# Decay masks added by accumulating DMAs, weight splits on one engine, four decay buffers and a bias table written in four DMAs

## The chip, the cores and the metric

The kernel runs on one core of one Trainium2 chip. The metric is the device time of one execution in microseconds (us); less is better. The instructions of the five engines (PE multiplies matrices, DVE and ACT work on vectors, POOL is the general engine, SP only issues DMAs) and of the DMA queues are put in a fixed order when the kernel is built: a scheduler of the kernel's framework orders each engine's list, and each engine then runs its list from the front and waits on semaphores. An instruction that waits holds up all that stand behind it on its engine.

## The reference

Two layers, each of a feed-forward block, a mixer and a second feed-forward block, on 512 tokens of 1024 features in float32:

```
for l in range(DEPTH):                                   # DEPTH = 2
    x = x + 0.5 * swiglu_ffn(rms_norm(x), w_gate, w_up, w_down)      # inner width 2816
    x = x + hybrid_mixer(rms_norm(x), ...)
    x = x + 0.5 * swiglu_ffn(rms_norm(x), w_gate, w_up, w_down)

hybrid_mixer: proj = h @ w_in, split into three branches; their outputs side by side @ w_out
  mLSTM, 4 heads of 64:   d[t, s] = exp(b[t] - b[s] + i[s] - m[t]) where s <= t, else 0
                          num = (q @ k.T * d) @ v,  h = num / max(|row sum|, exp(-m))
  SSM, 8 heads of 64:     depthwise convolution of 4 taps, then in blocks of 128 tokens
                          seg[l, s] = exp(a[l] - a[s]) where s <= l, else 0
                          y = (C @ B.T * seg) @ x + carried state
  attention, 4 heads:     softmax(q1 @ k1.T + bias) - lam * softmax(q2 @ k2.T + bias), causal
                          bias[h, t, s] = rel_bias[bucket(t - s), h]
```

## The kernel before

A weight arrives as float32 in tiles of 1 MiB named `raw` (two buffers, loaded on SP's queue, L107) and is split into a rounded part `whi` (ACT, L120) and a remainder `wlo` (L121), three buffers each. Each product of a weight block is then three matmuls (L126 to L128) with the activations' parts `xh` and `xl`. The first feed-forward block loads `wgu` (gate and up) and `wdn`; one `wgu` tile gives 48 matmuls.

The mixer's projections come from the tiles `win` (token-major) and `winf` (feature-major). Their splits go through `msplit` (L298): every third one has its subtraction on POOL, the others on DVE.

The attention works on two pairs of heads (p = 0, 1), four blocks of 128 queries and two heads: 16 steps, each with `soft` (logits by PE L523, bias and minimum by DVE L527, exponential by ACT L530, the two softmaxes joined by DVE L534 to L536), `turn` (transposes by PE L544, copied by ACT L546) and `weigh` (PE L555, DVE L559 and L560). At a pair's first step `load_pair` fetches the stacked queries and keys `st` (six DMAs of 256 KB from `qk_dram`, on POOL's queue, L503) and the bias tile T (L509). T is read from `bias_dram`, which `build_bias` (L239) fills once, in the first feed-forward block: a row of 640 values per head, four rows on four partitions, each written 128 times by one DMA on POOL's queue (L252).

The SSM has four decay tiles `sS` (two heads each, 128x1024) and the mLSTM four decay tiles `D`. An `sS` tile is a row of `row_dram` broadcast over the partitions by a DMA on SP's queue (L629), then POOL adds the causal mask `mask8` (L631), ACT takes eight exponentials (L636), DVE multiplies by the products `pG` (L638) and PE uses the tile (L643). A `D` tile is built in `decay` (L736) from a broadcast row `mb`: POOL adds the mask to four diagonal blocks (L742), ACT takes ten exponentials (L745), `scores` multiplies by `q @ k.T` (PE L755, DVE L756), `value` uses it (PE L764). The tiles T of the two pairs, `sS` 0 to 3 and `D` 0 to 3 take turns in one buffer ring, in that order:

```
        def big(name):
            return mp.tile([P, 1280], F32, name=name, tag="big", bufs=2)
```

Between PE's attention instructions the scheduler puts matmuls of projections for which weights are ready; these are called fillers below. The norms of the heads (`rstd`, L142 to L155) are short chains of small DVE operations.

Of the kernel before, what the change touches and what calls it, by code (L numbers as in the profile page):

```python
# [10 lines left out]
F32 = mybir.dt.float32  # L11
# [3 lines left out]
ALU = mybir.AluOpType  # L15
# [4 lines left out]
P = 128  # L20
# [9 lines left out]
NREL = 640  # L30

# columns of the per-feature vectors, per layer
PV_N1, PV_NM, PV_N2, PV_YW, PV_CW, PV_CB, PV_Q, PV_K, PV_N = 0, 8, 16, 24, 32, 64, 72, 73, 74
# columns of the vectors that every partition holds, per layer
BC_GB, BC_AL, BC_D, BC_LAM, BC_N = 0, 16, 24, 32, 160
# columns of the token-major groups of w_in
WIN_Q = KD * 272
WIN_Z, WIN_V, WIN_O = WIN_Q + 4096, WIN_Q + 8192, WIN_Q + 10240
# columns of the constants
# [4 lines left out]
def hybrid_kernel(ctx, tc, aps, phases):  # L44
# [25 lines left out]
    # ---- residual stream, feature-major  # L70
# [29 lines left out]
    # ---- weights: 1 MiB transfers, split into two float32r parts  # L100
# [29 lines left out]
    # ---- norm of the residual: the gain goes into the operand, the rms is divided out after the product  # L130
# [11 lines left out]
    def rstd(ssq, n):  # L142
        # (ssq / n + eps) ** -0.5 in place: a first guess from the exponent's bits, then Newton steps to float32
# [28 lines left out]
    # ---- SwiGLU  # L172
    def ffn(l, which, nxt, first):
        with tc.tile_pool(name=f"g{l}{which}", bufs=1) as gp:
            gh, gl = [], []
            for f in range(KF):
                if f == 0:
                    # gate and up in step, so that the parts of x are not all needed at once
# [22 lines left out]
                if f == 4 and first:  # L201
                    build_bias()
# [30 lines left out]
    # ---- negated bias of the relative positions: row q holds q + 384 - c at column c  # L233
# [5 lines left out]
    def build_bias():  # L239
        with tc.tile_pool(name="bb", bufs=1) as bp:  # L240
            oh = bp.tile([33, NREL], F32, name="oh")
            nc.sync.dma_start(out=oh, in_=aps["oh"])
            rb = bp.tile([33, 4], F32, name="rb")
            dve.memset(rb, NEG)
            nc.sync.dma_start(out=rb[0:32], in_=aps["rel_bias"])
            dve.tensor_scalar(rb, rb, -1.0, None, ALU.mult)
            row = bp.tile([4, NREL], F32, name="row")
            for a, b in ((0, 320), (320, 640)):
                ps = aux()
                pe.matmul(ps[0:4, :b - a], rb, oh[:, a:b], start=True, stop=True)  # L250
                dve.tensor_copy(row[:, a:b], ps[0:4, :b - a])
            pool.dma_start(out=bias_dram, in_=row[:, None, :].broadcast_to([4, P, NREL]))  # L252

    def mixer(l, nxt):
        pvl, bcl = l * PV_N, l * BC_N
        mp = ctx2.enter_context(tc.tile_pool(name=f"mx{l}", bufs=1))
        # slots of 2 and 8 KiB, each with the tiles that take turns in it
# [14 lines left out]
        def t2(name):  # L272
# [3 lines left out]
            # where the stacked queries and keys of the attention were  # L276
# [11 lines left out]
        def big(name):  # L288
            return mp.tile([P, 1280], F32, name=name, tag="big", bufs=2)

        # pairs of token blocks, 256 columns each
# [4 lines left out]
        npiece = [0]  # L296

        def msplit(raw, lo, n):  # L298
            npiece[0] += 1
            return split(raw, lo, n, pool if npiece[0] % 3 == 0 else dve)  # L300

        def token_proj(first, n, mid=None):
            # columns of one group, token-major, all token blocks at once; two blocks of 256 share a bank
# [23 lines left out]
        def feat_proj(i):  # L327
            # 128 columns, feature-major
# [13 lines left out]
        # ================= values of the attention, gates  # L342
# [12 lines left out]
        # difference weight of the attention  # L355
# [19 lines left out]
        # ================= queries and keys of the attention  # L375
# [14 lines left out]
        # the parts of a query over those of a key: one product of depth 96 for high x high + high x low + low x high  # L390
# [12 lines left out]
        # ================= gates: log1p(u) = 2 artanh(u / (2 + u))  # L403
# [17 lines left out]
        # log forget gates and dt * A side by side  # L421
# [10 lines left out]
        # sums up to a token, after it, and over its block  # L432
# [8 lines left out]
        # negated rows of the SSM's sums  # L441
# [16 lines left out]
        # ---- weights of the mLSTM's sources  # L458
        # log weight of source token s for a target block I, and the start value of its running maximum
# [33 lines left out]
        # ================= differential attention, two heads at a time, with negated logits  # L493
# [18 lines left out]
        def soft(n):  # L512
# [19 lines left out]
            # p1 / s1 - lam * p2 / s2, times -s1  # L532
# [38 lines left out]
        # ================= SSM: convolved inputs, feature-major  # L571
        # silu(x) = h * (1 + tanh(h)), h = x / 2: the taps are halved
# [46 lines left out]
        # decay of the SSM inside a block, log weights above the diagonal hidden  # L619
        for g in range(2):  # L620
# [4 lines left out]
            for pr_i in (2 * g, 2 * g + 1):  # L625
# [3 lines left out]
                nc.sync.dma_start(out=both.rearrange("p (h n) -> p h n", n=S), in_=src.broadcast_to([P, 2, S]))  # L629
                # the sources after a target, in its own block  # L630
                pool.tensor_tensor(blocks(both, P), blocks(both, P), mask8, ALU.add)  # L631
# [16 lines left out]
        # states before blocks 1..3, [state, head, 64], and what they give  # L648
# [29 lines left out]
        def head_norm(Y2, name):  # L678
            # rms over each head's 64 columns
# [26 lines left out]
        # gate and norm of the SSM  # L706
# [24 lines left out]
        # ================= mLSTM  # L731
        off = (0, 512, 896, 1152)
# [3 lines left out]
        def decay(h):  # L736
            mb = mp.tile([P, S], F32, name="row", tag="row", bufs=2)
            nc.sync.dma_start(out=mb, in_=row_dram[l, h:h + 1, :].broadcast_to([P, S]))
            D = big("D")
            for j in range(NB):  # L740
                d = slice(off[j], off[j] + P)
                pool.tensor_tensor(D[:, d], mb[:, j * P:(j + 1) * P], cn[:, CN_MSK:CN_MSK + P], ALU.add)  # L742
                for n in range(j, NB):
                    t = slice(off[j] + (n - j) * P, off[j] + (n - j + 1) * P)
                    act.activation(D[:, t], D[:, d] if n == j else mb[:, n * P:(n + 1) * P],  # L745
                                   AF.Exp, bias=G[:, 4 * j + n, h:h + 1], scale=-1.0)
            wD[h] = D

        def scores(h):
            hp = slice((h % 2) * 64, (h % 2) * 64 + 64)  # L750
            D = wD[h]
            for j in range(NB):
# [3 lines left out]
                dve.tensor_tensor(D[:, off[j]:off[j] + n], sp[:, :n], D[:, off[j]:off[j] + n], ALU.mult)  # L756

        def value(h):
# [3 lines left out]
            for n in range(NB):  # L762
                for j in range(n + 1):
                    pe.matmul(pnv[:, n, :], D[:, off[j] + (n - j) * P:off[j] + (n - j + 1) * P], V[:, j, h, :],  # L764
# [41 lines left out]
        # ================= output projection  # L806
# [35 lines left out]
    for n, (kind, l) in enumerate(phases):  # L842
# [3 lines left out]
        if kind == "mx":  # L846
            if n == 0:
                build_bias()
# [9 lines left out]
def _bucket_rows():  # L858
    # one row per bucket, a last one for the positions that the mask hides; column u is relative position 511 - u
# [21 lines left out]
def layout(inp):  # L881
# [6 lines left out]
    def cols(w, n):  # L888
        # [L, K, n*128] -> [L, n, 128 (k), K/128, 128]
# [66 lines left out]
```

## Time and profile before

| | |
|---|---|
| median of 3 runs | 2031.26 us (2027.05 to 2032.02) |
| span of the profiled execution | 2028.7 us |
| own time of the profiled execution beside its span | not given; the span is 2.56 us below the median of the runs |
| PE busy in the span | 1990.6 us (98%) |
| DVE, ACT, POOL busy | 1014.5, 700.9, 110.1 us |
| granted clock of PE, mean | 0.992 of full speed |

The span runs from the first to the last instruction. The stretches spoken of below are the first feed-forward block (to 385 us), mixer 1 (385 to 672 us), the two feed-forward blocks between the mixers (672 to 1388 us), mixer 2 (1388 to 1676 us) and the last feed-forward block (to the end).

### The profile page before, as it was taken

What the parts mean: (1) busy time and instruction counts of PE and PEld (TensorE: products, weight loads), DVE (VectorE), ACT (ScalarE), POOL (GpSimd) and SP (SyncE); (2) the same over time, 40 slices, a digit from 0 to 9 for tenths busy, and PEclk for the clock granted to TensorE, in tenths of its full rate; (3) what the DMA queues carried; (4) which work ended last, traced back from release to release, by engine and by line L of the source; (5) the groups of instructions that cost most, each with busy time, mean ns of one, the idle gap of its engine ahead of it and who ended that gap; (6) DMA issues with size and microseconds to landing.
All of it is one profiled execution on the core that took longest, in us unless ns stands there. A gap on an engine that the chain in (4) does not pass through costs nothing.

```text
span 2028.7 us, 23646 instructions
## 1 busy us (share of the span) xinstructions
PE 1990.6 (98%) x9654; PEld 1662.2 (82%) x9654; DVE 1014.5 (50%) x1659; ACT 700.9 (35%) x1144; POOL 110.1 (5%) x133
## 2 busy tenths in 40 slices
PE   8999999999899999999999999999998999999999
PEld 6878888978788888888888888889787888888887
DVE  6444433478766444443344444333876754444321
ACT  5223222345554333222232332223464533332211
POOL 0000000132210000000000000001222100000000
PEclk9999999999999999999999999999998999999999
DMA  5332222344212222222222222223532022222321
GB/s 177 95 118 83 104 103 85 118 144 127 83 52 81 86 104 85 103 104 83 104 84 103 104 84 104 103 75 122 159 110 88 32 99 89 104 85 103 109 99 62
DMA packets 35064, 200.73 MB, mean 99 GB/s; under 512 B 5179, under 2 KB 5467, under 8 KB 14092
## 3 DMA queue, kind: packets, MB, share of 16 engines
q1 hardware_dynamic: 29756, 185.28, 26.2%
q0 software_dynamic: 5200, 13.95, 2.8%
q8 instruction: 75, 1.23, 0.2%
q14 instruction: 33, 0.27, 0.0%
HBM read 191.56 MB, written 7.65 MB: 98 GB/s over the span
## 4 chain that ended last, share of the span: by engine, by line
PE 92%; DVE 4%; DMA 3%; ACT 1%; issue 1%; SPq 0%; POOL 0%; ACTq 0%; DVEq 0%; POOLq 0%
PE acc L126 16%; PE acc L128 16%; PE acc L127 16%; PE aux L126 12%; PE aux L128 12%; PE aux L127 12%; DMA raw<-wgu 3%; PE aux L764 1%; PE aux L643 1%; PE po L555 1%; PE po L755 0%; PE aux L544 0%; PE aux L523 0%; PE side L755 0%; ACT whi L120 0%
## 5 line engine op out<-in xcount | busy, mean ns | idle before, releaser
L120 ACT CAST whi<-raw 128x1024 fp32r<-128x1024 f32 (+2 forms) x344 | 350.8, 1022 | 994.2 <-PE acc L127 407.3
L121 DVE TENSOR_TENSOR wlo<-raw,whi 128x1024 fp32r<-128x1024 f32 (+1 forms) x326 | 386.2, 1187 | 346.1 <-ACT whi L120 345.6
L126 PE MATMUL acc<-xh,whi 128*128 128x512 f32 x896 | 353.1, 394 | 12.8 <-ACT xh L133 8.2
L127 PE MATMUL acc<-xl,whi 128*128 128x512 f32 x896 | 352.5, 393 | 0.0
L128 PE MATMUL acc<-xh,wlo 128*128 128x512 f32 x896 | 352.3, 393 | 0.1
L126 PE MATMUL aux<-xh,whi 128*128 128x512 f32 x704 | 274.2, 389 | 0.0
L128 PE MATMUL aux<-xh,wlo 128*128 128x512 f32 x704 | 274.1, 389 | 0.0
L127 PE MATMUL aux<-xl,whi 128*128 128x512 f32 x704 | 274.1, 389 | 0.0
L126 PEld LDWEIGHTS acc<-xh,whi 128*128 128x128 f32 x896 | 169.4, 189 | 47.3 <-ACT xh L133 8.2
L128 PEld LDWEIGHTS acc<-xh,wlo 128*128 128x128 f32 x896 | 169.1, 189 | 34.7 <-DVE wlo L121 1.1
L127 PEld LDWEIGHTS acc<-xl,whi 128*128 128x128 f32 x896 | 169.4, 189 | 34.0 <-DVE xl L134 0.4
L207 DVE TENSOR_TENSOR us<-aux,rsb 128x512 f32<-128x512 f32 x88 | 60.8, 691 | 265.7 <-PE aux L128 265.7
L127 PEld LDWEIGHTS aux<-xl,whi 128*128 128x128 f32 x704 | 132.3, 188 | 27.6
L128 PEld LDWEIGHTS aux<-xh,wlo 128*128 128x128 f32 x704 | 132.3, 188 | 27.5
L126 PEld LDWEIGHTS aux<-xh,whi 128*128 128x128 f32 x704 | 132.3, 188 | 27.4
L204 DVE TENSOR_TENSOR gs<-acc,rsb 128x512 f32<-128x512 f32 x88 | 60.8, 691 | 176.4 <-PE acc L128 172.5
L126 PE MATMUL acc<-gh,whi 128*128 128x512 f32 x352 | 138.7, 394 | 0.0
L126 PE MATMUL aux<-gh,whi 128*128 128x512 f32 x352 | 138.7, 394 | 0.0
L128 PE MATMUL acc<-gh,wlo 128*128 128x512 f32 x352 | 138.0, 392 | 0.0
L128 PE MATMUL aux<-gh,wlo 128*128 128x512 f32 x352 | 138.0, 392 | 0.0
L127 PE MATMUL acc<-gl,whi 128*128 128x512 f32 x352 | 136.6, 388 | 0.0
L127 PE MATMUL aux<-gl,whi 128*128 128x512 f32 x352 | 136.6, 388 | 0.0
(265 smaller groups left out, 2668.4 us busy)
## 6 DMA issues: line engine op xcount, KB each, us to landing
raw<-wgu SPq DMA_DIRECT2D x87, 1024.0 KB, 4.8
raw<-wdn SPq DMA_DIRECT2D x44, 1024.0 KB, 4.8
raw<-win SPq DMA_DIRECT2D x12, 1024.0 KB, 4.9
raw<-winf SPq DMA_DIRECT2D x12, 1024.0 KB, 4.9
raw<-wout SPq DMA_DIRECT2D x8, 1024.0 KB, 4.8
st<-qk_dram POOLq DMA_DIRECT2D x24, 256.0 KB, 5.4
qk_dram<-hl POOLq DMA_DIRECT2D x16, 256.0 KB, 3.3
sS<-row_dram SPq DMA_DIRECT2D x8, 512.0 KB, 4.4
```

Of the source, the lines that this page charges most:

```text
L120: act.copy(hi[:, t], raw[:, lo:lo + n])
L121: eng.tensor_tensor(lw[:, t], raw[:, lo:lo + n], hi[:, t].bitcast(F32), ALU.subtract)
L126: pe.matmul(out, lh, rh, start=first, stop=False)
L127: pe.matmul(out, lh, rl, start=False, stop=False)
L128: pe.matmul(out, ll, rh, start=False, stop=last)
L204: dve.tensor_tensor(gs, pp[0], rsb, ALU.mult)
L207: dve.tensor_tensor(us, pp[1], rsb, ALU.mult)
L555: pe.matmul(po[:, h * 64:(h + 1) * 64], at["a", n][:, j * P:(j + 1) * P], dv[j][:, (2 * p + h) * 64:(2 * p + h + 1) * 64], start=j == 0, s ...
L643: pe.matmul(py[:, j * P + hh * 64:j * P + hh * 64 + 64], sS[:, hh * S + j * P:hh * S + (j + 1) * P], XC[:, j, h * 64:(h + 1) * 64], start= ...
L764: pe.matmul(pnv[:, n, :], D[:, off[j] + (n - j) * P:off[j] + (n - j + 1) * P], V[:, j, h, :], start=j == 0, stop=j == n)
```

## The change

Four things change, and the order of all engines with them. The line numbers of the changed kernel are one to eleven higher than those of before.

1. The buffer ring `big` has four buffers in place of two.
2. All mixer splits have their subtraction on DVE.
3. The mask goes into `sS` and `D` by a DMA on SP's queue that copies it from the constants in SBUF (L631, L748 of the changed kernel), and the row is added to it by a DMA on POOL's queue that accumulates (L632, L749). POOL's 40 additions are gone. `D` has its four diagonal blocks side by side at the front now, so the multiplication in `scores` is one operation for the diagonal block and one for the rest: 7 in place of 4 for a head. The broadcast row `mb` is still loaded for the other blocks.
4. The bias table is written by four DMAs of one head each, called for at the tiles f = 3, 5, 7 and 9 of the first feed-forward block (before: one DMA, called for at f = 4), from the same four partitions.

```diff
+NBIG = 4
...
-                if f == 4 and first:
-                    build_bias()
+                if first and 3 <= f <= 9 and f % 2:
+                    build_bias(f // 2 - 1)
...
-            pool.dma_start(out=bias_dram, in_=row[:, None, :].broadcast_to([4, P, NREL]))
+    bias_row = const.tile([4, NREL], F32, name="bias_row")
...
+        pool.dma_start(out=bias_dram[h:h + 1], in_=bias_row[h:h + 1, None, :].broadcast_to([1, P, NREL]))
...
-            return mp.tile([P, 1280], F32, name=name, tag="big", bufs=2)
+            return mp.tile([P, 1280], F32, name=name, tag="big", bufs=NBIG)
...
         def msplit(raw, lo, n):
-            npiece[0] += 1
-            return split(raw, lo, n, pool if npiece[0] % 3 == 0 else dve)
+            return split(raw, lo, n)
...
-                nc.sync.dma_start(out=both.rearrange("p (h n) -> p h n", n=S), in_=src.broadcast_to([P, 2, S]))
-                # the sources after a target, in its own block
-                pool.tensor_tensor(blocks(both, P), blocks(both, P), mask8, ALU.add)
+                nc.sync.dma_start(out=blocks(both, P), in_=mask8)
+                pool.dma_start(out=both.rearrange("p (h n) -> p h n", n=S), in_=src.broadcast_to([P, 2, S]),
+                               accum_op=ALU.add)
...
+            nc.sync.dma_start(out=blocks(D[:, 0:S], P), in_=cn[:, None, CN_MSK:CN_MSK + P].broadcast_to([P, NB, P]))
+            pool.dma_start(out=D[:, 0:S], in_=row_dram[l, h:h + 1, :].broadcast_to([P, S]), accum_op=ALU.add)
             for j in range(NB):
-                d = slice(off[j], off[j] + P)
-                pool.tensor_tensor(D[:, d], mb[:, j * P:(j + 1) * P], cn[:, CN_MSK:CN_MSK + P], ALU.add)
...
-                dve.tensor_tensor(D[:, off[j]:off[j] + n], sp[:, :n], D[:, off[j]:off[j] + n], ALU.mult)
+                dve.tensor_tensor(D[:, at_(j, j)], sp[:, :P], D[:, at_(j, j)], ALU.mult)
+                if n > P:
+                    t = slice(off[j], off[j] + n - P)
+                    dve.tensor_tensor(D[:, t], sp[:, P:n], D[:, t], ALU.mult)
```

In POOL's list the four bias DMAs stand one behind the other, and only the first has something to wait for (the row on the four partitions). PE's small matmuls that make this row stand 48 matmuls earlier than before.

**PE, the second pair of heads in mixer 1's attention.** A row is an instruction: its line, its output and inputs by the program's names, the shape of what streams, and how often it stands there. `st` are the stacked queries and keys, `pt` a softmax, `aT` its transpose, `acc` a projection's bank. Before, near the pair's second query block:

```order
L544 MATMUL aux<-cn,pt 128x128
L523 MATMUL aux<-st 128x256 x2
L127 MATMUL acc<-xl_98,whi 128x512
L128 MATMUL acc<-xh_90,wlo 128x512
L555 MATMUL po<-dv_2602,aT 128x64
L126 MATMUL acc<-xh_91,whi 128x512
L127 MATMUL acc<-xl_99,whi 128x512
L128 MATMUL acc<-xh_91,wlo 128x512
L126 MATMUL acc<-xh_92,whi 128x512
```

The same place in the changed kernel:

```order
L545 MATMUL aux<-cn,pt 128x128
L524 MATMUL aux<-st 128x256 x2
L556 MATMUL po<-dv_2605,aT 128x64
L545 MATMUL aux<-cn,pt 128x128 x2
L524 MATMUL aux<-st 128x384 x2
L556 MATMUL po<-dv_2605,aT 128x64 x2
```

In the changed kernel this pair has no fillers from its first logits to its last but one transposes, in mixer 1 alone; mixer 2's two pairs have some between most steps, as before. The fillers that stood there now stand in the first pair of mixer 1 (72 matmuls of three `winf` halves), and the first pair's start has moved behind both `z` projections.

**ACT, the first pair of mixer 1's attention.** `L` are the logits, `nacs` the bias of the SSM's exponentials. Before, the pair's second and third query blocks:

```order
L530 ACTIVATE pt,sm<-L,mx 128x256 x2
L546 COPY aT<-aux 128x256
L587 ACTIVATE rw<-CT_3783 128x512
L530 ACTIVATE pt,sm<-L,mx 128x384
L546 COPY aT<-aux 128x256
```

The same place in the changed kernel:

```order
L531 ACTIVATE pt,sm<-L,mx 128x256
L547 COPY aT<-aux 128x256
L638 ACTIVATE sS<-sS,nacs 128x128 x4
L531 ACTIVATE pt,sm<-L,mx 128x384
L638 ACTIVATE sS<-sS,nacs 128x128
L531 ACTIVATE pt,sm<-L,mx 128x384
L547 COPY aT<-aux 128x256
```

The exponentials of the first two SSM decay tiles have moved between those of the first pair, and those of the third tile between those of the second pair; before, the first decay tile's stood in the second pair and the others behind the attention. The fourth tile's stand behind the attention in both.

**SP, the loads around mixer 1's attention.** `winf` with the mLSTM's queries and keys is loaded in two tiles, `win` here is the mLSTM's values and gate. Before:

```order
L107 DMA raw<-winf 128x2048 x2
L629 DMA sS<-row_dram 128x1024
L107 DMA raw<-win 128x2048 x2
L629 DMA sS<-row_dram 128x1024
L107 DMA raw<-wout 128x2048
L629 DMA sS<-row_dram 128x1024 x2
```

In the changed kernel:

```order
L108 DMA raw<-winf 128x2048
L745 DMA row<-row_dram 128x512
L108 DMA raw<-win 128x2048
L631 DMA sS<-cn 128x8x128 x2
L108 DMA raw<-win 128x2048
L631 DMA sS<-cn 128x8x128
L108 DMA raw<-wout 128x2048
L631 DMA sS<-cn 128x8x128
```

The first two fills with the mask stand behind the load of the values' weights, which needs the `raw` buffer of the first `winf` tile; the third and fourth wait for the buffers of the two pairs' T. In mixer 2 the first two fills stand ahead of the `z` weights and of all `winf` tiles.

## Rows read from the trace of the kernel before

**Rows 1.** The page's head and its busy times by engine.

```profile
span 2028.7 us, 23646 instructions
PE 1990.6 (98%) x9654; PEld 1662.2 (82%) x9654; DVE 1014.5 (50%) x1659; ACT 700.9 (35%) x1144; POOL 110.1 (5%) x133
```

**Rows 2.** Waits of PE: engine, line, releaser, us in total, times, longest.

```profile
PE aux L544 <- DVE pt L536: 7.4, 6, 1.7
...
PE aux L643 <- DVE sS L638: 6.9, 2, 3.5
PE acc L126 <- ACT whi L120: 4.6, 1, 4.6
PE aux L394 <- DVE qk L389: 4.4, 2, 2.2
```

**Rows 3.** Windows: stretch, length, busy us of each engine (instructions), PE clock, DMA share, GB/s.

```profile
385.00:672.00 287.00, 276.33 (x1651) 238.06 (x1650) 199.95 (x453) 139.35 (x312) 50.47 (x53) 0.98 0.31 102
560.00:570.00 10.00, 10.00 (x57) 9.95 (x57) 3.05 (x5) 3.12 (x10) 2.07 (x5) 0.63 0.32 105
672.00:1388.00 716.00, 716.00 (x3174) 591.84 (x3175) 307.06 (x375) 210.38 (x259) 3.61 (x7) 1.00 0.27 95
1560.00:1570.00 10.00, 8.46 (x39) 8.46 (x40) 5.10 (x7) 3.59 (x12) 2.04 (x5) 0.54 0.32 105
```

**Rows 4.** DMA issues of the whole span: count, KB each, median us to landing.

```profile
raw<-wgu SPq DMA_DIRECT2D x87, 1024.0 KB, 4.8
...
st<-qk_dram POOLq DMA_DIRECT2D x24, 256.0 KB, 5.4
...
sS<-row_dram SPq DMA_DIRECT2D x8, 512.0 KB, 4.4
...
bias_dram<-row POOLq DMA_DIRECT2D x1, 1280.0 KB, 56.5
```

**Rows 5.** The chain of work through the bias DMA, 66 to 130 us: start, us, what.

```profile
103.11 22.67 DMA raw<-wgu
```

**Rows 6.** DMA view of 60 to 140 us in 40 slices: busy tenths of 16 engines, GB/s.

```profile
DMA  0086013178222584222222972298222222028308
GB/s 0 0 242 283 0 11 30 20 151 293 26 34 26 75 284 145 56 58 54 57 53 58 245 228 26 26 203 249 23 55 60 65 78 86 0 33 348 143 16 319
```

**Rows 7.** Groups of POOL's instructions by shape, whole span.

```profile
L121 POOL TENSOR_TENSOR wlo<-raw,whi 128x1024 fp32r<-128x1024 f32 x16 | 38.7, 2417 | 147.8 <-ACT whi L120 126.4 <-PE aux L544 21.4
L631 POOL TENSOR_TENSOR sS<-sS,cn 128x1024 f32<-128x1024 f32 x8 | 20.9, 2613 | 48.3 <-DMA sS<-row_dram 44.0 <-DVE rs_q L154 4.2
```

**Rows 8.** Timeline of DVE beside a POOL split that starts at 423.93 us.

```profile
423.76 0.22 DVE L154 SCALAR_TENSOR_TENSOR rs_q<-rs_q,rs_v 128x64 f32<-128x64 f32 x1
424.01 2.40 DVE L155 SCALAR_TENSOR_TENSOR ssq<-rs_q,ssq 128x64 f32<-128x64 f32 x1
```

**Rows 9.** Groups of DVE's, then PE's attention instructions in mixer 1 (385 to 672 us).

```profile
L527 DVE CUSTOM_DVE_ANT_0 L<-aux,T 128x128 f32<-128x128 f32 (+3 forms) x32 | 15.2, 483 | 5.0 <-PE aux L523 4.4 <-ACT pt L530 0.4
L536 DVE SCALAR_TENSOR_TENSOR pt<-pt,ka 128x128 f32<-128x128 f32 (+3 forms) x16 | 10.9, 680 | 0.1
...
L535 DVE SCALAR_TENSOR_TENSOR ka<-sm,lam,ka 128x1 f32<-128x1 f32 x16 | 4.6, 290 | 0.1
...
L527 DVE DVE_READ_ACCUMULATOR2_ANT mx<- 128x1 f32 x32 | 2.6, 82 | 0.0
...
L534 DVE RECIPROCAL ka<-sm 128x1 f32<-128x1 f32 x16 | 2.5, 158 | 0.7 <-ACT pt L530 0.5
...
L555 PE MATMUL po<-dv,aT 128*128 128x64 f32 x80 | 11.6, 276 | 0.2 <-ACT aT L546 0.2
...
L523 PE MATMUL aux<-st 96*128 96x128 f32 (+3 forms) x32 | 9.1, 350 | 0.0
L544 PE MATMUL aux<-cn,pt 128*128 128x128 f32 x40 | 7.2, 279 | 3.7 <-DVE pt L536 3.7
```

**Rows 10.** The chain of work behind mixer 1's attention, 545 to 572 us.

```profile
551.69 2.41 POOL sS L631
```

More of the change, by code (lines that the diff above doesn't have):

```diff
@@ L237, in hybrid_kernel, with build_bias @@
     qk_dram = dram.tile([2, 2, 2, 4, 32, S], F32, name="qk_dram")
[L239 to L251, printed above, removed]
-            pool.dma_start(out=bias_dram, in_=row[:, None, :].broadcast_to([4, P, NREL]))
+    bias_row = const.tile([4, NREL], F32, name="bias_row")
+    def build_bias(h):
+        if h == 0:
+            with tc.tile_pool(name="bb", bufs=1) as bp:
+                oh = bp.tile([33, NREL], F32, name="oh")
+                nc.sync.dma_start(out=oh, in_=aps["oh"])
+                rb = bp.tile([33, 4], F32, name="rb")
+                dve.memset(rb, NEG)
+                nc.sync.dma_start(out=rb[0:32], in_=aps["rel_bias"])
+                dve.tensor_scalar(rb, rb, -1.0, None, ALU.mult)
+                for a, b in ((0, 320), (320, 640)):
+                    ps = aux()
+                    pe.matmul(ps[0:4, :b - a], rb, oh[:, a:b], start=True, stop=True)
+                    dve.tensor_copy(bias_row[:, a:b], ps[0:4, :b - a])
+        pool.dma_start(out=bias_dram[h:h + 1], in_=bias_row[h:h + 1, None, :].broadcast_to([1, P, NREL]))
     def mixer(l, nxt):
@@ L294, in pair @@
             return t, [t[j // 2][:, (j % 2) * 256:(j % 2) * 256 + 256] for j in range(NB)]
-        npiece = [0]
         def msplit(raw, lo, n):
-            npiece[0] += 1
-            return split(raw, lo, n, pool if npiece[0] % 3 == 0 else dve)
+            return split(raw, lo, n)
         def token_proj(first, n, mid=None):
@@ L729, in mixer, with at_ @@
             transpose_out(k, lambda j: YS[:, j, (k - 2) * P:(k - 1) * P], y8[:, k - 2])
-        off = (0, 512, 896, 1152)
+        off = (512, 896, 1152)
+        def at_(j, n):
+            c = j * P if n == j else off[j] + (n - j - 1) * P
+            return slice(c, c + P)
         Ym2, Ym = pair("Ym")
@@ L739, in decay @@
             D = big("D")
+            nc.sync.dma_start(out=blocks(D[:, 0:S], P), in_=cn[:, None, CN_MSK:CN_MSK + P].broadcast_to([P, NB, P]))
+            pool.dma_start(out=D[:, 0:S], in_=row_dram[l, h:h + 1, :].broadcast_to([P, S]), accum_op=ALU.add)
             for j in range(NB):
-                d = slice(off[j], off[j] + P)
-                pool.tensor_tensor(D[:, d], mb[:, j * P:(j + 1) * P], cn[:, CN_MSK:CN_MSK + P], ALU.add)
                 for n in range(j, NB):
-                    t = slice(off[j] + (n - j) * P, off[j] + (n - j + 1) * P)
-                    act.activation(D[:, t], D[:, d] if n == j else mb[:, n * P:(n + 1) * P],
+                    act.activation(D[:, at_(j, n)], D[:, at_(j, n)] if n == j else mb[:, n * P:(n + 1) * P],
                                    AF.Exp, bias=G[:, 4 * j + n, h:h + 1], scale=-1.0)
@@ L763, in value @@
                 for j in range(n + 1):
-                    pe.matmul(pnv[:, n, :], D[:, off[j] + (n - j) * P:off[j] + (n - j + 1) * P], V[:, j, h, :],
+                    pe.matmul(pnv[:, n, :], D[:, at_(j, n)], V[:, j, h, :],
                               start=j == 0, stop=j == n)
@@ L847, in hybrid_kernel @@
             if n == 0:
-                build_bias()
+                for h in range(4):
+                    build_bias(h)
             with ExitStack() as ctx2:
@@ L945 @@
     arrays = layout(inputs)
-    nc = bacc.Bacc("TRN2", target_bir_lowering=False, num_devices=1)
+    nc = bacc.Bacc("TRN2", target_bir_lowering=False, num_devices=1, dynamic_dma_scratch_size=4096)
     aps = {}
```

## The prediction

> **What bounds the kernel now.** The page comes first: PE is busy for 1990.6 of 2028.7 us [rows 1], so the kernel is bound by PE, and an edit on another engine gains only where PE stands idle, at most 38 us in all. PE's waits say where that is [rows 2]: 7.4 us before the attention's transposes (L544) for DVE's L536, 6.9 before the SSM products (L643) for L638, 4.6 once in the first feed-forward block for the cast of a weight, and 4.4 before the transposes of the queries for L389. The windows agree: 716 of 716 us in the blocks between the mixers, 276.33 of 287 in mixer 1 [rows 3]. A second loss doesn't show as idle time: behind the long wait before L643 PE is busy with a granted clock between its two levels of half and full speed, 0.63 (10.00 of 10 us, mixer 1) and of 0.54 (8.46 of 10, mixer 2) [rows 3], which costs 10 x 0.37 = 3.7 and 10 x 0.46 = 4.6 us. Everything below is about these waits, and about new ones like them. The sum is made against the span; the median of the runs lies 2.56 us above it, and I add that at the end.
>
> **Bias table.** The DMA of 1280 KB takes 56.5 us to land, a weight tile of 1024 KB 4.8 [rows 4]. Where it runs alone, the DMA engines are busy for 2 tenths and move 26 GB/s; with a weight load's tail beside it 53 to 58 [rows 6], so the load gets some 30. Loads then take 22.67 us [rows 5], twice in a row (the other 22.80), together 36 us late, and the price was one wait of 4.6: the buffers hold some 31 us of lead.
>
> The table still comes from the same four partitions. Two bounds. If 26 GB/s is the limit of the source, the four DMAs still need 1.31 MB / 26 GB/s = 50 us, but now on more engines, and each weight load meets them in all its parts. PE uses a tile in 48 matmuls of 716 / 3174 = 0.226 us [rows 3], 10.8 us, so it wants 4.6 tiles in those 50 us and gets 50 x 30 GB/s = 1.4; it falls 3.2 x 10.8 = 34 us behind, 3 to 4 more than the lead. Were packets to alternate one for one over the whole 51 us, one tile would come 46 us late: a wait of 15. So 4.6 becomes between 3.5 and 15. If, on the other side, the limit was the few engines, the table clears in some ten us and the 4.6 goes. I take the source limit, and +3, because 26 GB/s is so far below 218 (1 MiB in 4.8 us); bounds -4.6 and +10.
>
> The Trainium skill (SBUF — State Buffer, section on Door 1, the DMA port swizzle) says that partitions 0 to 3 hang on one DMA port of 27.2 GB/s; the 26 of the slices agrees, and by that rule the four DMAs would need 48 us on whatever engines. The same notes (DMA: Bandwidth & Descriptors, how many engines a DMA uses) let the dimension of 4 in the old DMA give four engines and the 128 of the new ones sixteen; the 2 tenths agree with the four, and no run here shows the sixteen. By both rules together the weights are hindered on every engine, which speaks against this edit.
>
> **POOL's tensor work on the way of DVE.** 16 large splits of 2.42 and 8 mask additions of 2.61 us leave POOL [rows 7]. Beside such a split a DVE operation took 2.40 us where its neighbour of the same shape took 0.22 [rows 8], so each can hold DVE for two us, and I put the longest waits before L544, 1.7 us in each mixer, down to that [rows 2]. Against that DVE gets 18 splits of about 1.2, eleven us in each mixer. Before the attention the two about cancel: -0.5 in each mixer, bounds 0 and -2.2 (the wait for L389). In mixer 2's second pair the 1.7 goes.
>
> **Mixer 1, first pair.** The exponentials of the first decay tile now stand between the exponentials of the attention in ACT's list, and whatever is behind them waits until that tile is filled and accumulated. SP's list has the fill behind the load of the values' weights, which needs the `raw` buffer that is freed at about the pair's start. From there: 2 us for that split, 4.8 for the load, some 2 more for the fill beside it (4.4 alone), then an accumulation that no row of before shows. Its nearest rows: the same 512 KB from the same rows by a plain DMA, 4.4, and two of POOL's loads of 256 KB, 10.8 [rows 4]. I take 5.4, nearer to the plain one. That makes 14 us. ACT's list reaches the place behind 27 fillers and the first steps of the pair, some 7.5 us in. ACT waits about 6, PE's instructions behind it a little less: +5, bounds 0 (the load lands earlier) and +8.
>
> **Mixer 1, second pair.** PE's list has no fillers there [the rows of PE's list shown with the change]. A pair costs DVE (15.2 + 10.9 + 4.6 + 2.6 + 2.5) / 2 = 17.9 us, 17 without the held one, and PE (11.6 + 9.1 + 7.2) / 2 = 14.0 [rows 9]; so at least 3 us of idle time, which the fillers covered before. On top, `st` of this pair is loaded when the first pair's last logits are done: six issues of half a microsecond and 5.4 to land [rows 4] against some 27 fillers (6.1 us), so 3 more at the start, and the steps wait for each other's chain. Bounds +3 and +9, taken +6. The displaced fillers are no gain, they filled the first pair. And idle PE was followed by a lower clock above: 2.5 more, bounds 0 and 5.
>
> **The tails.** In both mixers the wait of about 3.45 before L643 ended with POOL's mask addition of 2.41 us [rows 2, 10], behind which stood ACT's and DVE's steps. Three of the four tiles are ready long before now, so it goes, and with it the 3.7 and the 4.6 of low clock. What is late next is D: its buffers come free when the SSM products are done, then fill (4.4 or less), issue and accumulation follow, and ACT's exponentials of the diagonal stand ahead of the copies that PE's state products need. I put 1.5 on it in each mixer, bounds 0 and 4. The split multiplications of `scores` (12 more small DVE operations a mixer) lie beside full PE work; without it, some 0.3 us each.
>
> **Sum.** Mixer 1: -0.5 + 5 + 6 + 2.5 - 3.45 - 3.7 + 1.5 = +7.3. Mixer 2, where fillers and early fills stay: -0.5 - 1.7 - 3.5 - 4.6 + 1.5 + 1 (DVE's added splits between the steps) = -7.8. Bias +3. Together +2.5: a span of 2031.2, a time of 2033.8 us, said as 2034. That is no change by 0.3% (6 us), which is about what a measurement here can tell.
>
> **Rivals.**
> A, the bias on all engines: packets alternate one for one, PE waits 15 instead of 4.6, so 7 above my +3, and a low clock behind it 2: 2043. For it the 22.67 us of a load that met the table on few engines only; against it that the issue may spread the four over time. It decides once a `wgu` load takes over 45 us.
> B, the bias is quick: 4.6 gone instead of +3, 7.6 less, 2026. For it: 26 GB/s may belong to the few engines. Against: a lone weight load gets 13 GB/s from each of sixteen, and the table got 6.5 from each of four or so.
> C, slow accumulation: 10.8 us instead of 5.4 for the first tile puts 5 more on ACT's wait in mixer 1, and some 3 on D in each mixer, 2045. For it, it reads and writes the tile; against, only one tile per mixer is on the path.
> The Trainium skill lists accumulation among what POOL's software queue alone does (DMA: Bandwidth & Descriptors, rules for kernel authors); no row of before shows its time.
> D, the unfilled pair costs nothing: the steps overlap as they did before and the first pair finds its tile ready; -11 in mixer 1's terms, 2023. The 3 us floor speaks against it.
>
> **Chances.** Forecast 0.42 (its own range 2027 to 2041), A 0.18, B 0.18, C 0.15, D 0.07. A and C are slower by over 0.3% for the most part (0.29 of 0.33), B is split about evenly at the bound (0.10 faster), D is faster; of the forecast's own spread 0.09 lies slower and 0.03 faster. So faster 0.20, same 0.42, slower 0.38. The range takes in A, B and nearly all of C: 2020 to 2048.
>
> **What the profile of the changed kernel would show.** Right: four bias DMAs of some 50 us in all and `wgu` loads of over 22 us beside them, with one or two waits of PE of 4 to 8 us by 130 us; no wait of PE at L643's line behind the attention, and clock 1.0 there; idle time of PE inside the second pair of mixer 1, before transposes and logits, and ACT waiting for the accumulation in the first; mixer 2 with some 10 us less idle time than mixer 1. Wrong: bias DMAs that land within 15 us; accumulations beyond 10 us; D's wait behind the SSM over 4 us; or DVE as the releaser in mixer 2's pairs, which would mean that the splits cost more than POOL's hold did.

## The result and the profile after

The changed kernel takes 2050.75 us (median of 4 runs, 2049.02 to 2057.6), the kernel before 2030.55 on the same chip: a ratio of 1.0105, interval 1.0087 to 1.0124. The forecast was no change, 2034 us, in a range to 2048; it is slower by 20 us.

Where the 20 us lie is read off the timelines by marks that both kernels have: DVE's last update of x in a feed-forward block, and its first gate multiplication in the block behind a mixer.

| stage | before, us | after, us | difference | forecast |
|---|---|---|---|---|
| first feed-forward block, to its last update of x | 381.3 | 399.8 | +18.5 | +3 |
| mixer 1, to the next block's first gate | 292.4 | 309.7 | +17.3 | +7.3 |
| two feed-forward blocks between | 711.0 | 711.0 | 0 | 0 |
| mixer 2, to the next block's first gate | 292.5 | 276.9 | -15.6 | -7.8 |
| the rest | 351.5 | 351.5 | 0 | 0 |
| span | 2028.7 | 2048.9 | +20.2 | +2.5 |

All the signs came as forecast, and each of the three sizes was forecast at about half of what was measured or less. The page of the changed kernel, to be held against [rows 1]:

```profile
span 2048.9 us, 23668 instructions
...
PE 1993.5 (97%) x9654; PEld 1663.1 (81%) x9654; DVE 995.9 (49%) x1701; ACT 699.2 (34%) x1144; POOL 48.9 (2%) x94
```

PE is busy for only 2.9 us more than before, so over the whole span the loss is idle time. Its waits (engine, line, releaser, us in total, times, longest; `issue` says that the profile shows nothing that the engine waited for), to be held against [rows 2]:

```profile
PE acc L127 <- ACT whi L121: 22.1, 1, 22.1
...
PE aux L524 <- issue: 6.4, 1, 6.4
PE po L556 <- ACT aT L547: 5.1, 6, 2.3
PE aux L545 <- DVE pt L537: 2.4, 2, 1.6
PE aux L475 <- DVE Gm L467: 1.9, 1, 1.9
```

The three large waits of the mixers in [rows 2] are gone or small. One wait for the cast of a weight has grown from 4.6 to 22.1 us, and there is a new one of 6.4 us before logits. The windows show what that one brings (stretch, length, busy us by engine, clock, DMA share, GB/s). The first and last are mixer 1 and mixer 2 between the marks of the table:

```profile
399.80:709.50 309.70, 290.24 (x1692) 248.10 (x1691) 196.44 (x486) 142.18 (x320) 23.19 (x43) 0.94 0.38 109
540.00:550.00 10.00, 3.60 (x21) 2.75 (x19) 1.68 (x3) 1.93 (x3) 1.67 (x3) 0.82 1.08 238
550.00:560.00 10.00, 7.33 (x30) 6.03 (x29) 5.98 (x30) 6.55 (x26) 0.00 (x0) 0.50 0.37 95
560.00:570.00 10.00, 7.44 (x29) 5.66 (x27) 7.03 (x27) 5.70 (x17) 0.00 (x0) 0.50 0.00 1
570.00:580.00 10.00, 9.27 (x32) 7.51 (x31) 5.60 (x14) 3.00 (x7) 0.89 (x1) 0.50 0.28 66
1420.40:1697.40 277.00, 275.24 (x1692) 238.31 (x1691) 194.38 (x487) 142.06 (x320) 22.93 (x41) 1.00 0.41 122
```

The two mixers between the same marks before:

```profile
381.30:673.70 292.40, 281.73 (x1692) 243.32 (x1691) 204.76 (x465) 142.99 (x320) 53.66 (x62) 0.98 0.32 102
1384.70:1677.20 292.50, 281.79 (x1692) 243.41 (x1691) 204.97 (x465) 143.07 (x320) 53.97 (x62) 0.98 0.31 101
```

From 540 to 550 us PE works for 3.60 us; for the next 30 it runs at a clock of 0.50, the lower of its two levels, with 6 us of gaps in all. Of the 17.3 us that mixer 1 lost, 8.5 are the same number of matmuls that keep PE busy longer, at a mean clock of 0.94 in place of 0.98, and 8.8 are idle time (19.5 against 10.7). Mixer 2 is the opposite: PE is idle for 1.8 us of it, at clock 1.00.

The chain through the bias DMAs and their rows (issues; count, KB each, median us to landing), against [rows 5] and [rows 4]:

```profile
65.67 45.94 DMA raw<-wgu
```

```profile
st<-qk_dram POOLq DMA_DIRECT2D x24, 256.0 KB, 6.2
...
sS<-row_dram POOLq DMA_DIRECT2D x8, 512.0 KB, 6.3
...
D<-row_dram POOLq DMA_DIRECT2D x8, 256.0 KB, 5.0
...
bias_dram<-bias_row POOLq DMA_DIRECT2D x4, 320.0 KB, 32.4
```

and the DMA engines from 50 to 160 us in 40 slices of 2.75 us, against [rows 6]:

```profile
DMA  0373979999997988999995404637003800270037
GB/s 0 69 319 11 32 22 26 28 30 46 54 52 56 67 54 54 53 54 60 70 74 207 191 9 125 256 48 334 0 0 54 334 0 0 66 316 0 0 48 334
```

Here the reader sees where the first loss comes from: from 61 to 108 us all engines are busy, mostly for nine tenths or more, at 22 to 74 GB/s. One weight tile takes 45.94 us in place of 4.8, and the busy share says nothing of what is moved.

### The profile page after: what moved, and what is told of

The parts are those of the page before. It is cut to its first block, busy times and chain, and to the rows that moved or that the text cites. A ratio compares the mean times of both kernels' runs of the same rounds, so it can differ in the third digit from the quotient of the medians.

```text
span 2048.9 us, 23668 instructions
## 1 busy us (share of the span) xinstructions
PE 1993.5 (97%) x9654; PEld 1663.1 (81%) x9654; DVE 995.9 (49%) x1701; ACT 699.2 (34%) x1144; POOL 48.9 (2%) x94
## 4 chain that ended last, share of the span: by engine, by line
PE 93%; DMA 4%; DVE 1%; ACT 1%; issue 0%; SPq 0%; ACTq 0%; POOLq 0%; DVEq 0%
PE acc L127 17%; PE acc L129 17%; PE acc L128 17%; PE aux L127 12%; PE aux L129 12%; PE aux L128 12%; DMA raw<-wgu 2%; PE aux L774 1%; PE po L556 1%; PE po L762 1%; PE aux L645 1%; PE aux L545 0%; DMA sS<-cn 0%; DMA D<-cn 0%; PE aux L524 0%
## 5 line engine op out<-in xcount | busy, mean ns | idle before, releaser
L122 DVE TENSOR_TENSOR wlo<-raw,whi 128x1024 fp32r<-128x1024 f32 (+2 forms) x344 | 407.5, 1187 | 370.0 <-ACT whi L121 369.6
L127 PE MATMUL acc<-xh,whi 128*128 128x512 f32 x896 | 354.0, 395 | 30.4 <-ACT whi L121 22.1
```

What stands on the lines that cost most here:

```text
L122: eng.tensor_tensor(lw[:, t], raw[:, lo:lo + n], hi[:, t].bitcast(F32), ALU.subtract)
L127: pe.matmul(out, lh, rh, start=first, stop=False)
```

## The experiments

**1. One bias DMA again.** In the changed kernel `build_bias` is called at f = 4 alone and writes the table with the old DMA; all else stays.

```diff
-                if first and 3 <= f <= 9 and f % 2:
-                    build_bias(f // 2 - 1)
+                if first and f == 4:
+                    build_bias(0)
...
-        pool.dma_start(out=bias_dram[h:h + 1], in_=bias_row[h:h + 1, None, :].broadcast_to([1, P, NREL]))
+        pool.dma_start(out=bias_dram, in_=bias_row[:, None, :].broadcast_to([4, P, NREL]))
```

> The changed kernel with the bias table written by one DMA at f = 4 as before. Theory: the four DMAs cost 18.5 us in the first feed-forward block, and through the order that the scheduler made with them 17.3 us in mixer 1, while the other three parts gain 15.6 in each mixer. Then this runs in 2050.8 - 18.5 - 17.3 - 15.6 = about 1999 us, with one wait of PE of 4 to 5 us for a weight cast and mixer 1 as short as mixer 2. Rival, the prediction's own: mixer 1 loses by the accumulations and the pair without fillers, whatever the bias does; then only the 18.5 go, about 2032 us.

Measured: 2001.86 us, ratio 0.9859 (0.9844 to 0.9874). PE's waits have the cast at 4.9 us, and both mixers take 277.3 us by the marks (660.6 - 383.3 and 1648.8 - 1371.6):

```profile
PE acc L127 <- ACT whi L121: 4.9, 1, 4.9
PE aux L662 <- ACT bt L659: 1.7, 2, 1.0
PE aux L675 <- ACT st L666: 1.6, 2, 1.0
```

So beside the other three parts the edit of the bias table costs 49 us, and only 16.5 of them (399.8 - 383.3) in the block where it runs; the other three parts alone gain 29 (2031.08 to 2001.86). In the changed kernel the four DMAs had landed by about 111 us, and mixer 1 begins at 400; what the edit changed there is the order. POOL's list has the loads of T ahead of everything else of the mixer in this version, and behind the queries' and keys' loads in the changed one:

```
one DMA:                                  four DMAs:
L256 DMA bias_dram<-bias_row 512x1x640    L256 DMA bias_dram<-bias_row 128x1x640 x4
L462 MEMSET Gm 128x64                     L402 DMA qk_dram<-hl (8 rows)
L469 MEMSET Ps 128x4                      L448 DMA row_dram<-ar 8x512
L510 DMA T<-bias_dram 128x512 x4          L462 MEMSET Gm 128x64
L802 MEMSET V 128x4 x4                    L469 MEMSET Ps 128x4
L402 DMA qk_dram<-hl (8 rows)             L504 DMA st<-qk_dram 32x4x512 x2
L448 DMA row_dram<-ar 8x512               L485 DMA row_dram<-mr 4x128 x4
L504 DMA st<-qk_dram 32x4x512             L504 DMA st<-qk_dram 32x4x512 x4
L485 DMA row_dram<-mr 4x128 x4            L510 DMA T<-bias_dram 128x512 x4
```

In PE's list the pairs of mixer 1 have 91 and 45 filler matmuls between their first and last logits here, as those of mixer 2; in the changed kernel 51 and none. That the scheduler reckoned with a table that is written much later than it is would explain it; the lists show the displacement, its reason inside the scheduler is argued. Four bias DMAs alone do not bring it: in experiments 2 and 4 the pairs of mixer 1 keep their fillers (92 and 38, 91 and 45).

**2. The four DMAs in the kernel before.** `build_bias` and its calls as in the changed kernel, in the kernel before (with the smaller scratch space for DMAs, which makes room for the row).

> The kernel before with the four bias DMAs alone (two buffers, POOL's splits and masks as before; the scratch space for DMAs made smaller as in the changed kernel, since the row needs room). In POOL's list three of the four stand together and the fourth behind the mixer's first split. Theory: three quarters of the bytes hold the weight loads for some 38 us on all engines: a wait of about 34 + 5 - 31 = 8 to 10 us for a cast in place of 4.6, and no change in the mixers beyond 2: 2034 to 2040 us. Rival: if the 22.1 us of the changed kernel came from its DVE splits or its other order, nothing changes here: 2030.

Measured: 2039.06 us, ratio 1.0042 (1.0027 to 1.0057). The wait for the cast is 10.1 us, the other waits are those of [rows 2]:

```profile
PE acc L126 <- ACT whi L120: 10.1, 1, 10.1
...
PE aux L547 <- DVE pt L539: 7.4, 6, 1.7
PE aux L646 <- DVE sS L641: 7.0, 2, 3.5
```

and the slow weight load in the chain of work (start, us, what):

```profile
65.09 33.85 DMA raw<-wgu
```

The loss in the first block needs nothing of the change but these DMAs, and it goes with the bytes that stand together: three of them give 10.1, four gave 22.1. Mixer 1 takes 294.7 us, 2.3 more than before, against the 17.3 more of the changed kernel.

**3. The table from DRAM.** The four rows go to a tile of 10 KB in DRAM, and four DMAs write the table from there. As in experiment 1, `build_bias` is called at f = 4 alone.

```diff
+    bias_small = dram.tile([4, NREL], F32, name="bias_small")
...
-        pool.dma_start(out=bias_dram[h:h + 1], in_=bias_row[h:h + 1, None, :].broadcast_to([1, P, NREL]))
+        pool.dma_start(out=bias_small, in_=bias_row)
+        for k in range(4):
+            pool.dma_start(out=bias_dram[k], in_=bias_small[k:k + 1, :].broadcast_to([P, NREL]))
```

> The changed kernel with the four rows first written to a small tile in DRAM (10 KB) and the table then written by four DMAs from there, DRAM to DRAM, each row broadcast 128 times. Theory (the limit of 26 GB/s is that of the four source partitions): the four DMAs land within some 10 us in all, no wait of PE for a cast, 4.6 us and its low clock better than with one DMA: about 1994 us. Rival (the limit lies with the rows' size, the destination or POOL's queue): they take some 50 us here too, and the wait for the cast is 15 to 22 us: 2010 to 2017.

Measured: 1993.01 us, ratio 0.9817 (0.9801 to 0.9834), the fastest version of the study. The same 1280 KB to the same place, 4.8 us each:

```profile
bias_dram<-bias_small POOLq DMA_DIRECT2D x4, 320.0 KB, 4.8
...
bias_small<-bias_row POOLq DMA_DIRECT2D x1, 10.0 KB, 2.0
```

The first feed-forward block ends at 374.5 us by the marks, 6.9 before the kernel before's. Destination, row size and POOL's queue are out as the limit.

**4. The same four DMAs, far apart.** Each reads a copy of the rows that DVE makes for it; the copies share one place, so each waits for the DMA before.

```diff
+        with tc.tile_pool(name=f"own{h}", bufs=1) as op:
+            own = op.tile([4, NREL], F32, name="own")
+            dve.tensor_copy(own, bias_row)
-        pool.dma_start(out=bias_dram[h:h + 1], in_=bias_row[h:h + 1, None, :].broadcast_to([1, P, NREL]))
+            pool.dma_start(out=bias_dram[h:h + 1], in_=own[h:h + 1, None, :].broadcast_to([1, P, NREL]))
```

> The changed kernel, but each of the four bias DMAs reads its own copy of the rows, which DVE makes when the copy of the DMA before has been read, so that they start far apart (the first near f = 4, the last behind the first feed-forward block). Theory: each still reads one partition at about 26 GB/s and takes 327680 / 26 GB/s = 12.6 us on all engines, but the weights' lead of 31 us covers each by itself: no wait for a cast, about 1994 to 1996 us. Rival: if sixteen engines together draw more than 26 GB/s when nothing is queued behind them, they land in 5 us; if the hold of the engines costs in proportion wherever it lies, waits of some 4 us stand behind each of them: 2010.

Measured: 2013.01 us, ratio 0.9915 (0.99 to 0.9929), 17 to 19 us above the sum that was expected, while the first block, which the experiment was about, came as expected. The DMAs took 13.8 us each, 24 GB/s, and the first block ends at 374.7 us with no wait for a cast: three of them beside weight loads cost nothing. But the fourth was issued at 389.96 us, and the mixer's small tiles, which reuse the copy's place, waited for it (PE's wait, then POOL's):

```profile
PE acc L127 <- DVE cwh L578: 16.8, 1, 16.8
```

```profile
POOL Gm L465 <- DMA bias_dram<-own: 13.3, 1, 13.3
```

That explains 16.8 of the 17 to 19 us; it comes from where the copy lies, not from the DMAs' pace.

**5. Rows on four ports.** The version of experiment 1 with one DMA of the same shape, whose four source rows lie on partitions 0, 4, 8 and 12.

```diff
+                rs = bp.tile([33, 16], F32, name="rs")
+                dve.memset(rs, 0.0)
-                dve.tensor_scalar(rb, rb, -1.0, None, ALU.mult)
+                dve.tensor_scalar(rs[:, 0:16:4], rb, -1.0, None, ALU.mult)
...
-                    pe.matmul(ps[0:4, :b - a], rb, oh[:, a:b], start=True, stop=True)
+                    pe.matmul(ps[0:16, :b - a], rs, oh[:, a:b], start=True, stop=True)
...
-        pool.dma_start(out=bias_dram, in_=bias_row[:, None, :].broadcast_to([4, P, NREL]))
+        pool.dma_start(out=bias_dram, in_=bias_row[0:16:4, None, :].broadcast_to([4, P, NREL]))
```

> The version with one bias DMA (2001.9 us), its four rows now on partitions 0, 4, 8 and 12 in place of 0 to 3; the DMA has the same shape, bytes and engines. Theory: what limits it is a path that the neighbouring partitions 0 to 3 share, some 26 GB/s; the rows on four separate paths give each engine its own rate, at most 4 x 26: 1.31 MB in 13 to 20 us, no wait for the cast, 1995 to 1996 us. Rival: the limit is the four engines or the row's size: it lands after 57 us as before and the wait of 4.9 stays, 2002 us.

Measured: 1993.75 us, ratio 0.9821 (0.9807 to 0.9836). It lands after 18.7 us instead of 57.5, and where no weight load runs beside it (the slices of 2 us from 72 to 76 us and at 86 us) it moves 95 to 105 GB/s, four times the 26 of [rows 6], on the same two tenths of the engines but for its first slice:

```profile
bias_dram<-bias_row POOLq DMA_DIRECT2D x1, 1280.0 KB, 18.7
```

```profile
DMA  0059004269422287000591002750005900028300
GB/s 0 0 74 442 8 0 95 105 162 353 143 106 114 105 227 307 0 0 0 74 401 49 0 0 33 283 217 0 0 0 135 385 4 0 0 33 340 152 0 0
```

This settles the disputed price. The Trainium skill (SBUF — State Buffer, section on Door 1, the DMA port swizzle) gives partitions 0 to 3 one port and partitions 4, 8 and 12 others, 27.2 GB/s each; 26 for one and 105 for four agree with it.

**6. Masks on POOL, with the four DMAs.** The changed kernel with the old code for the masks of `sS` and `D` (and the old layout of `D`), no accumulating DMA. PE's list has mixer 1's second pair without fillers, as the changed kernel's.

> The changed kernel with its four bias DMAs, but the masks added by POOL and no accumulating DMA. Its list for PE has mixer 1's second pair without fillers as the changed kernel's. Theory: mixer 1 loses by that order (late start, no fillers, the wait for the stacked keys, the low clock behind it), not by accumulations: against the same version with the table from DRAM (2006.3 us) it is 25 us longer in the first feed-forward block and 27 to 33 longer in mixer 1, 2058 to 2064 us. Rival, the prediction's +5 for ACT behind the accumulation and its slow sibling: that part goes, mixer 1 is 15 to 25 longer, 2046 to 2056.

Measured: 2059.52 us, ratio 1.0144 (1.0129 to 1.0159). Against the same version with the table from DRAM (experiment 8) the first block is 25.5 us longer by the marks and mixer 1 28.2, inside the theory's bounds. Its waits include 5.3 us before the second pair's logits for the keys and queries. So mixer 1's loss comes without accumulating DMAs, and it comes with that order.

**7 to 9. One of the other three parts undone, in the version with the table from DRAM.** In 7 `NBIG = 2`; in 8 the masks as in 6; in 9 every third split back on POOL:

```diff
-            return split(raw, lo, n)
+            npiece[0] += 1
+            return split(raw, lo, n, pool if npiece[0] % 3 == 0 else dve)
```

> The version with the table written from DRAM (1993.0 us), with two buffers in the ring in place of four; splits on DVE and masks by DMA stay. Theory: the tails behind the attention (a wait of 3.45 us before the SSM products and some 4 us of low clock in each mixer) came from tiles that had to wait for the buffers of T, so they come back: 12 to 18 us more, 2005 to 2011. Rival: they came from POOL's mask addition in the chain, which is gone here; then about 1995.

> The version with the table written from DRAM, with the masks added by POOL as before (rows loaded by SP's queue, the old layout of D); four buffers and the splits on DVE stay. Theory: with four buffers the additions come early, so the tails stay away; POOL's eight additions of 2.6 us hold a DVE operation now and then, 1 to 4 us in each mixer: 1995 to 2001. Rival: the accumulating DMAs are what removed the tails; then 8 us in each mixer come back, about 2009.

> The version with the table written from DRAM, with every third mixer split on POOL as before; four buffers and the masks by DMA stay. Theory: POOL's splits hold DVE's two-input operations for two us each, and the waits before the transposes of the queries (2.2 and a lower clock), the attention's transposes (up to 3.7) and the convolution's (1.0) come back in each mixer: 5 to 9 us each, 2003 to 2011. Rival, the prediction's -0.5: what DVE gets back it pays for the nine splits it takes over; then 1992 to 1996.

Measured: two buffers 2017.32 us (ratio 0.9937, 0.9922 to 0.9952), masks on POOL 2006.3 (0.9893, 0.9873 to 0.9912), splits on POOL 2013.29 (0.9916, 0.9901 to 0.993). Each costs more than expected: 24.3, 13.3 and 20.3 us against 1993.01. PE's waits for two buffers, then for splits on POOL:

```profile
PE aux L648 <- DVE sS L643: 7.1, 5, 2.7
PE aux L665 <- ACT bt L662: 4.4, 2, 3.3
```

```profile
PE aux L401 <- DVE qk L396: 4.5, 2, 2.2
PE aux L551 <- DVE pt L543: 3.5, 4, 1.4
...
PE side L631 <- DVE CT L595: 2.3, 2, 1.1
PE side L611 <- DVE rw L586: 2.0, 2, 1.0
```

With two buffers the wait before the SSM products is back, and nothing ahead of it changed: the first block ends 1.2 us later than with four, the second pair's last logits of mixer 1 too, and the last SSM product (L648) 13.3 us later (553.0 against 539.7). With the splits on POOL the waits before the queries', the attention's and the convolution's transposes are back. The theory named the right places and took too little for them; over both mixers PE is idle for 11, 7 and 13 us more than in experiment 3. With two buffers low clock adds to that (0.98 in both mixers); with masks or splits on POOL the clock stays at 1.00 and 0.99. The three sizes add up to 57.9 us, while all three parts together are worth 2025.69 - 1993.01 = 32.7 (experiment 10): undone one at a time they do not add, and every list has another order each time.

**10. The table from DRAM in the kernel before.**

> The kernel before with the table written from DRAM alone (and the smaller scratch space for DMAs). Theory: the wait of 4.6 us for the cast goes and the low clock behind it, 6.7 us as in the changed kernel's version, the mixers stay as they were: 2024 us. Rival: the mixers change too, since the row has another place; beyond 2 us either way.

Measured: 2025.69 us, ratio 0.9972 (0.9958 to 0.9985); the runs scatter more than others here, 2014.6 to 2029.28. In the profiled one the first block ends 6.5 us earlier and the mixers take 290.7 and 292.7 us, in place of 292.4 and 292.5.

**11. Splits on DVE alone.** The version of experiment 10 with `split(raw, lo, n, dve)` for all mixer splits.

> The kernel before with the table from DRAM (2025.7 us) and all splits on DVE; two buffers, masks on POOL. Theory: without POOL's splits the holds of DVE go that made PE wait before the transposes of the queries (2.2 and 1.7 of low clock in each mixer), before the convolution's (1.0) and in part before the attention's (2 of 3.7): 12 to 15 us less, 2011 to 2014. Rival, the prediction's -0.5 and -1.7: 2022 to 2025, the nine splits take back what DVE gains.

Measured: 2010.67 us, ratio 0.9899 (0.9883 to 0.9916), 15.0 less than experiment 10 by the medians and 10.1 by the profiled spans. The waits before the transposes of the queries, of the attention and of the convolution are gone; with two buffers and POOL's masks, 5.5 us before the SSM products stay. My -0.5 was the rival, and it fell.

## Why the prediction was wrong, point by point

**What bounds the kernel** held: PE's busy time differs by 3 us between the two kernels (8.5 more in mixer 1, 6.6 less in mixer 2), and each difference is a wait of PE or low clock behind one. Where PE waited before is where it gained.

**Bias table.** This step failed by size: +3 was taken, +18.5 measured, beyond the upper bound of +10, and rival A, with a wait of 15, was the right case with 22.1. The mechanism was the one that the step gave (one source path of 26 GB/s, now on all engines); experiment 5 shows the path, experiment 2 that the DMAs do it alone. The 30 GB/s for weights beside the table was right too: from 65.67 us, when the late tile was issued, to 110 us SP's queue moved 1.34 MB and POOL's 1.15 (queue: packets, MB, share of 16 engines; then the weight loads of these 44 us):

```profile
q0 software_dynamic: 286, 1.15, 88.1%
q1 hardware_dynamic: 176, 1.34, 7.2%
...
raw<-wgu SPq DMA_DIRECT2D x2, 1024.0 KB, 41.8
```

The term that was mis-sized most is the lead of 31 us: it is 19. The tile landed 45.9 - 4.8 = 41 us late, and PE waited 22.1. Experiment 2 gives the same: 33.85 - 4.8 = 29 late, a wait of 10.1. The 31 came from adding the delays of two slow loads, 36 - 4.6, and these do not add: the second was issued at 103.1 us and landed at 125.8, while in experiment 3 the same load is issued at 97.3 and lands after 4.7. So it was 23.8 late, and 23.8 - 4.6 is 19 again. With a lead of 19 the 34 us of the step would have been a wait of 15. The other 7 us fit that two tiles shared the 1.34 MB: neither was there by 110 us, when the table was nearly written, and rival A's tile that comes 46 us late was as near to the 41 as the 34 was.

**POOL on the way of DVE.** Failed: -0.5 in each mixer and -1.7 in mixer 2. All three waits of this kind went, not one of them (2.2 + 3.7 + 1.0 us in each mixer before; the changed kernel has 2.4 us before L545, in mixer 1 alone), and experiment 11 gives 10 to 15 us for both mixers. The row of 2.40 us for 0.22 was read rightly; the error was to set the nine splits that DVE takes over against it. That these fall where DVE has time, while a hold falls on whatever DVE does then, would explain it; it is argued.

**Mixer 1, first pair.** The wait of ACT for the accumulation is there, 5.0 us in two pieces (L638), near the 6 said, and of PE's waits for ACT before L556 in this pair, 4.0 us in all, the longest is 2.3. The first tile's accumulation took 6.1 us, the median of all eight is 6.3, said 5.4. What failed here is "they filled the first pair", said of the displaced fillers: the first pair had more of them before. Counted in the traces from a pair's first logits to its last `weigh` product, the first pair has 70 in place of 239 and the second 17 in place of 64. They went ahead of both: 666 projection matmuls in place of 453 stand before the first logits, which come 114.5 us after the block's last update of x in place of 86.5.

**Mixer 1, second pair.** Right in kind, with the lower clock too small. The wait for `st` is 6.4 us (the view of the tile `st` names L524 as what waited for it), and the windows from 550 to 580 us have 6 us more of gaps, 12 in place of the 6 taken; the 30 us at half clock, with PE busy for 24 of them, are what the 2.5 should have been: an estimate from these windows is 24 / 2 = 12 us. Mixer 1 in whole lost less by the clock, since it had some 10 us of low clock before as well: PE is busy for 8.5 us longer.

What the prediction did not see is where this order came from. It read the lists as they stood, and so had the sign for mixer 1, but it put the bias edit at +3 and all of that into the first block. Experiment 1 shows that with one bias DMA mixer 1 has its fillers and takes 277.3 us like mixer 2. So 32 us in mixer 1 (309.7 - 277.3) come with the bias edit, and the rest of the change is worth 277.3 - 292.4 = -15.1 there. Rival D's mixer 1 (+7.3 - 11 = -3.7) was nearer to that than the forecast. The bias edit does it only together with some of the other parts: on the kernel before it costs mixer 1 2.3 us (experiment 2). Accumulating DMAs are not among the parts that it needs (experiment 6).

**The tails.** Right: no wait before the SSM products, clock 1.00. D costs less than the 1.5 said, 0.9 us before L662 in each mixer and 0.4 before L675 in one. Experiment 7 shows that the four buffers did it: with two the wait is back, though POOL's addition is gone. With four buffers and POOL's additions (experiment 8) 1.2 us of it are left.

**The rivals.** A came true in the first block. B's quick table is what experiments 3 and 5 make of it. C is out: 6.1 us for the first tile, where it said 10.8. The sum of the terms other than the bias was +1.7 measured and -0.5 forecast, which is chance: +17.3 and -15.6 were said as +7.3 and -7.8.

**Left open.** Why the scheduler puts T's loads so late with four DMAs, and which of the buffers and the splits it takes for that; and how the 57.9 us of experiments 7 to 9 split between waits and changed lists.

## What to carry to other kernels

A DMA's price is what it keeps from others, not its own landing: before a slow DMA is spread over more engines, its rate has to be known from where it runs alone, and which side limits it; here moving three source rows by a few partitions, or going through 10 KB of DRAM, was worth 8 to 9 us, and spreading it cost 16.5 in its own block. Count how late the tile is that the engine waits for; delays of loads in a row do not add. Then read the lists of all engines after any edit, also hundreds of microseconds behind it: here the loads and fillers moved some 400 us behind the edit, and that cost twice as much. And a wait of PE costs itself and the clock behind it: 10 us with little work were followed by 30 at half clock.

## What the runs showed of the hardware

- DMAs from one partition, or from four neighbouring ones, move 23 to 26 GB/s however many engines work on them (13.8 us for 320 KB, one such DMA at a time; 50 us for 1280 KB); the same DMA from partitions 0, 4, 8 and 12 moves 95 to 105 where no weight load runs beside it, and lands in 18.7 us.
- The busy share of the DMA engines does not tell what they move: nine tenths at 22 to 32 GB/s while the four DMAs run alone (61 to 75 us), two tenths at 26 with the one DMA before.
- The weights, 1 MiB in 4.8 us alone, got some 30 GB/s beside the four DMAs (1.34 MB in 44.3 us).
- Accumulating DMAs of 512 KB from DRAM into SBUF take 6.3 us in the median (4.9 to 13.2), of 256 KB 5.0, beside 4.4 and 3.9 for plain loads of these rows before; their issue takes POOL 0.9 us each instead of 0.55.
